# Seven products instead of eight for three more pairs of projection blocks, and z loaded from memory for every second attention head

## The chip, the cores and the metric

The kernel runs on one core of one Trainium2 chip. The metric is the device time of one execution in microseconds (us); the time before is the median of three runs. The core's engines are TensorE (PE in the rows, with its weight loads as PEld), VectorE (DVE), ScalarE (ACT), GpSimd (POOL) and SyncE (SP, which here issues nearly all DMAs). PE adds up its products in PSUM, eight banks of 128 x 512 float32.

## The reference, cut to what matters

```python
h = rmsnorm(x, norm_g)                       # 1024 tokens x 1024
proj = einsum('bsd,de->bse', h, w_in)        # 11280 columns
(a_q, a_k, a_v, a_o, a_z, a_g, b_q, b_k, b_v, b_z, g_a, g_b) = split(proj)
# branch A, mLSTM of 4 heads of width 256
qk = silu(conv5(concat(a_q, a_k)))
y_a = rmsnorm(mlstm_fw(qk, a_v, a_g) + mlstm_bw(qk, a_v, a_g)) * sigmoid(a_o) * silu(a_z)
# branch B, differential attention, 8 heads of width 128 (two score maps of width 64 each)
att = (softmax(q0 @ k0.T * s) - lam * softmax(q1 @ k1.T * s)) @ b_v      # q, k with RoPE
y_b = rmsnorm(att) * (1 - lambda_init) * silu(b_z)
mix = sigmoid(g_a + gb0) * (y_a @ w_branch_a) + sigmoid(g_b + gb1) * (y_b @ w_branch_b)
out = rmsnorm(x + mix @ w_out, final_g)
```

All of it is float32. The kernel reaches that precision with three products for one: each operand is split into a rounded part (names ending in H) and the rest (L), and H·H, H·L and L·H are added.

## The kernel before

**Blocks.** A block is 128 columns of the projection for all 1024 tokens. Done plainly (`proj`, L429) it is two halves of 512 tokens, each 8 contraction blocks x 3 products, so 48 matmuls of 128x512 into the PSUM tiles `pj`, of which there are two.

**Pairs.** Two blocks can be done together as a 2x2 block product with seven products in place of eight (Strassen's scheme in Winograd's form: `pair_units`, L291; the sums of weight blocks come from `load_form`, those of h from the opening, in `TH`/`TL`). A product is 4 contraction blocks x 3 matmuls, so a pair is 84 matmuls of 128x512 where two plain blocks are 96. A sink takes the four quarters of the result (block i, token half j). Sixteen pairs are made this way, all for the mLSTM: q and k (`conv_sink`) and o with z (`oz_sink`). Results leave for DRAM; their working tiles are the six buffers of `big` and six PSUM banks `T`.

**Stages, in order of time.** The opening: normalise, transpose, four gate blocks (branch B's gate, blocks 0 to 3). The sixteen pairs. A prologue of the attention (q, k, z of head 0 and v of heads 0 and 1). The attention's eight heads. Its tail, with gate blocks between. The mLSTM. The rest of the gates, the two branch products, the output.

**A head of the attention** is eight cycles t, one for 128 queries (`da_cycle`). On PE a cycle has S (12 score matmuls, L923, into two double-bank tiles `S` that fill all of S's banks), T (two groups of four transposes of the combined probabilities of the cycle before, L131 `T<-ident,e`), in odd cycles PV (two groups of 12 products, L959), in even ones M (two transposes of the result `att`, for its mean square), and in cycles 4 and 5 G (four transposes each of the row scale of the head before). T, PV, M and G share two PSUM banks, also called `T`. After S, VectorE takes two maxima `nm` (L926), ScalarE two exponentials `e` (L928), VectorE then combines them (L932 to L934). After T, ScalarE makes `pH` (L947) and VectorE `pL` (L948). After M, ScalarE squares (L971). In G the result is multiplied with `zg` = z(1+tanh(z/2)) (L880, L881) and stored to `yb`.

**The fill.** Between these units stand pieces of plain projection: q and k of the next head (`da_proj`; its results go through VectorE, GpSimd `m`, ScalarE `hl` and DMAs into `kst` and `qq`), v of the next two heads (`da_v`), z and gate blocks (`gate_units`). `Weaver.weave` merges the two lists by planned costs and lags; the tuple `FILL` says how many gate blocks a head gets.

**What sets the order.** PE's order is the one that the weaver writes. The other engines and the DMA queues are ordered by the scheduler of the framework, which reckons with costs of its own; each engine then executes strictly in that order.

Of the kernel before, what the change touches and what calls it, by code (L numbers as in the profile page):

```python
# [7 lines left out]
F32 = mybir.dt.float32  # L8
F32R = mybir.dt.float32r
I32 = mybir.dt.int32  # L10
AF = mybir.ActivationFunctionType
ALU = mybir.AluOpType
AX = mybir.AxisListType

S = 1024
# [3 lines left out]
NH_B = 8  # L19
# [15 lines left out]


INF = 1.0e9
FILL = (1, 0, 0, 0, 0, 0, 0, 3)
MM = 0.214
TP = 0.109  # L40

# [68 lines left out]
class Block:  # L110
# [202 lines left out]
    def oz_sink(self, i0):  # L313


        v, a, box = self.v, self.a, {}

        def sink(i, j, ps, rest):
            if "z" not in box:
                box["z"] = self.big("oz")  # L320
            z = box["z"][:, j * 512:(j + 1) * 512]
            first = j not in box
            box[j] = True
            if rest is not None:
                to = self.psA.tile([128, 512], F32, name="pj", tag="pj", bufs=2) if i == j == 1 else ps
                v.tensor_tensor(out=to, in0=ps, in1=rest, op=ALU.add)
                ps = to
            more = lambda out, x, y: v.scalar_tensor_tensor(out=out, in0=x, scalar=1.0, in1=y, op0=ALU.add, op1=ALU.mult)
            if i == 0:
                a.activation(out=z if first else ps, in_=ps, func=AF.Tanh, scale=0.5)  # L330
                if not first:
                    more(z, ps, z)
            else:
                th = self.s0.tile([128, 512], F32, name="tz", tag="tz", bufs=2)
                a.activation(out=th, in_=ps, func=AF.Tanh, scale=0.5)
                more(z if first else ps, th, ps)
                if not first:
                    more(z, z, ps)
            if not first:
                self.q.dma_start(out=self.gd_ml[i0][:, j * 512:(j + 1) * 512], in_=z)  # L340
        return sink

    def conv_sink(self, seg, n):

# [497 lines left out]
    def da_proj(self, h, st):  # L842
        A, v, a, p, q = self.A, self.v, self.a, self.p, self.q
        w1 = self.w1
        fb = lambda x: x.bitcast(F32)
        kA, kB = ("rope", h, 0), ("rope", h, 1)

        def first(half, pa):
            c = slice(half * 512, (half + 1) * 512)
            m = [w1.tile([128, 512], F32, name=f"m{i}", tag=f"m{i}", bufs=1) for i in range(2)]  # L850
            st["m"] = m
            v.tensor_tensor(out=m[0], in0=pa, in1=self.cosT[:, c], op=ALU.mult)
            v.tensor_tensor(out=m[1], in0=pa, in1=self.sinT[:, c], op=ALU.mult)

        def second(half, pb):
            c = slice(half * 512, (half + 1) * 512)
            if half == 0:
                st["k"] = w1.tile([128, 2, S], F32R, name="kst", tag="kst", bufs=2)
            qq = st["q", half] = w1.tile([128, 2, 512], F32R, name="qq", tag="qq", bufs=3)
            m = st["m"]  # L860

            hl = w1.tile([128, 4, 512], F32R, name="hl", tag="hl", bufs=1)
            v.tensor_tensor(out=fb(hl[:, 2]), in0=pb, in1=self.sinT[:, c], op=ALU.mult)
            v.tensor_tensor(out=fb(hl[:, 3]), in0=pb, in1=self.cosT[:, c], op=ALU.mult)
            p.tensor_tensor(out=m[0], in0=m[0], in1=fb(hl[:, 2]), op=ALU.subtract)
            p.tensor_tensor(out=m[1], in0=fb(hl[:, 3]), in1=m[1], op=ALU.add)
            for i in range(2):
                a.copy(hl[:, i, :], m[i])
                p.tensor_tensor(out=hl[:, 2 + i, :], in0=m[i], in1=fb(hl[:, i, :]), op=ALU.subtract)
            for x in range(2):  # L870
                for i, to in enumerate((st["k"][:, :, c], qq)):
                    for j in range(2):
                        r, g = 64 * j + 32 * x, 64 * (1 - i) + 32 * j
                        q.dma_start(out=fb(to[r:r + 32]), in_=fb(hl[g:g + 32, x::2]))

        kz = ("w_in", OFF["bz"] + 128 * h)

        def zz(half, ps):
            st["g", half] = g = w1.tile([128, 512], F32, name="zg", tag="zg", bufs=2)
            a.activation(out=g, in_=ps, func=AF.Tanh, scale=0.5)  # L880
            v.scalar_tensor_tensor(out=g, in0=g, scalar=1.0, in1=ps, op0=ALU.add, op1=ALU.mult)  # L881

        qk = []
        for half in range(2):
            qk += self.proj(kA, half, lambda ps, half=half: first(half, ps))
            qk += self.proj(kB, half, lambda ps, half=half: second(half, ps), name=("qk", h))
        z = self.proj(kz, 0, lambda ps: zz(0, ps)) + self.proj(kz, 1, lambda ps: zz(1, ps), name=("z", h))
        for half in range(2):
            z[(half + 1) * self.PIECES - 1].after = ((("G", h - 1, half), LAG["G"]),)
        return qk, z  # L890
# [538 lines left out]
    def build(self):  # L1429
# [19 lines left out]
        do = lambda f, cost=0.0: Unit(cost, f)  # L1449
        pool = lambda *x, **k: tc.tile_pool(*x, **k)  # L1450
        with pool(name="const", bufs=1) as self.const, \
# [16 lines left out]
            dt = lambda n: [self.dram.tile([128, S], F32, name=f"{n}{i}") for i in range(8)]  # L1468
            self.tg = {"ga": dt("tga"), "gb": dt("tgb")}
            self.ya, self.yb, self.gd_ml = dt("ya"), dt("yb"), dt("gm")  # L1470
            self.cd = {n: dt("c" + n) for n in ("ak", "akH", "akL", "aqH", "aqL")}
            self.pairs, sinks, self.praws, self.f = [], [], {}, {}
            for n in range(NH_A):
                for i, seg in enumerate(("ak", "aq")):
                    self.pairs.append(((seg, 2 * n), (seg, 2 * n + 1)))
                    sinks.append(self.conv_sink(seg, n))
                    self.pairs.append((("ao", 2 * n + i), ("az", 2 * n + i)))
                    sinks.append(self.oz_sink(2 * n + i))
            self.ident = self.const.tile([128, 128], F32, name="ident")
            make_identity(self.nc, self.ident)  # L1480
            self.mhalf = self.const.tile([128, 8], F32, name="mhalf")
            self.v.memset(self.mhalf, -0.5)

            gq = [("gb", i) for i in range(8)] + [("ga", i) for i in range(8)]
            fill = lambda m: sum((self.gate_units(*gq.pop(0)) for _ in range(m)), [])

            def begin():
# [12 lines left out]
            sts = [dict() for _ in range(NH_B)]  # L1500
            stm = [dict() for _ in range(NH_A)]
            st3 = {}
            w = Weaver()
            w.add(enter("h", "hpool"), enter("tab", "tab", side="right"), enter("tf", "tf", side="right"),
                  enter("p0", "p0", side="right"), banks("ps0", T=6), keep(E.PE, E.Activation, E.DVE, E.Pool), do(begin))
            k = self.PIECES
# [37 lines left out]
            w.add(leave("ps0", "s0", "tf"), enter("w1", "w1", side="right"), banks("ps1", S=2, T=2))  # L1544
            w.banks.update(S=1, T=2)
            qk, z = zip(*[self.da_proj(h, sts[h]) for h in range(NH_B)])
            w.add(do(lambda: setattr(self, "ahead", True)), *qk[0], *z[0], *self.da_v(0, sts[0:2]))
            prev = None
            for h in range(NH_B):
                cur = self.da_parts(h, sts[h])  # L1550
                main = sum((self.da_cycle(cur, prev, t) for t in range(8)), [])
                ahead = qk[h + 1] if h + 1 < NH_B else []
                if h + 1 == NH_B:
                    nxt = fill(FILL[h]) + z[h]
                elif h % 2 == 1:
                    nxt = ahead + self.da_v((h + 1) // 2, sts[h + 1:h + 3]) + fill(FILL[h])
                else:
                    nxt = z[h - 1] + ahead + fill(FILL[h]) + z[h] if h else ahead + fill(FILL[0])
                w.weave(main, nxt)
                prev = cur  # L1560
            end = sum((self.da_cycle(None, prev, t) for t in range(6)), [])
# [8 lines left out]
            rest = fill(len(gq))  # L1570
# [17 lines left out]
            k = len(passA) // 2  # L1588
# [52 lines left out]
```

## Time and profile before

| | |
|---|---|
| runs | 1705.68, 1709.62, 1704.77 us; median 1705.68 |
| the profiled execution | 1706.56 us in all, span 1704.7 us from first to last instruction |
| PE, DVE, ACT, POOL busy | 97%, 58%, 46%, 36% of the span |
| matmuls | 9431 |
| mean granted clock of TensorE | 0.994 |
| stages, us from the start | opening to 67; pairs 67 to 398; prologue to 455; heads 0 to 6 455 to 999; head 7 999 to 1067 (its last S); tail to 1124; mLSTM and the rest to 1705 |

The rows give a start and a length in us, the engine, the line of the code, the operation and its operands as out<-in, the shape, a count, and in brackets how long the engine had been idle and what ended that. A matmul's length is longer than its distance to the next one, since they are pipelined; for what one costs the distance counts.

### The profile page before, as it was taken

The numbers are of one execution on the slowest core, as the hardware profiler recorded it, in microseconds if no ns is written. First come the engines' busy times: TensorE is split into PE (matmuls) and PEld (weight loads), VectorE is DVE, ScalarE is ACT, GpSimd is POOL, SyncE is SP. The second block draws the span as 40 slices with busy tenths as digits, with TensorE's granted clock in tenths as the row PEclk, the third lists the DMA queues.
The fourth block names the chain that finished last, engine by engine and source line by source line (L and its number), as shares of the span: only waits on it lengthen the run. The fifth ranks groups of instructions, "written<-read, shape, count | busy, mean of one in ns | idle before, by whom it ended". The sixth has DMA issues, their size and how long they took to land. (4 is left out here: it accounts for less than half of the span.)

```text
span 1704.7 us, 25425 instructions
## 1 busy us (share of the span) xinstructions
PE 1654.3 (97%) x9431; PEld 1389.8 (82%) x9431; DVE 988.3 (58%) x1799; ACT 777.0 (46%) x1554; POOL 606.5 (36%) x680
## 2 busy tenths in 40 slices
PE   7999999999999999999999999999999899999998
PEld 5777887887877987898788878899999777888887
DVE  5778668674377666666666655226666633135533
ACT  7454555553265455454545455325655644022221
POOL 5767676665243134413241331221330312212000
PEclk9999999999999999999999999999999999999999
DMA  5334444334231213221231222175464327344222
GB/s 181 98 121 130 137 123 132 116 124 146 65 81 44 63 38 87 56 69 38 75 81 32 62 62 75 50 208 155 143 170 137 109 89 237 117 147 136 87 91 83
DMA packets 175630, 178.79 MB, mean 105 GB/s; under 512 B 12185, under 2 KB 135410, under 8 KB 175506
## 3 DMA queue, kind: packets, MB, share of 16 engines
q1 hardware_dynamic: 174594, 175.58, 34.5%
q8 instruction: 74, 1.21, 0.3%
q10 hardware_dynamic: 912, 1.59, 0.2%
q14 instruction: 50, 0.41, 0.1%
HBM read 114.11 MB, written 46.24 MB: 94 GB/s over the span
## 5 line engine op out<-in xcount | busy, mean ns | idle before, releaser
L429 PE MATMUL pj<-hH,wH 128*128 128x512 f32 x640 | 266.8, 417 | 3.3 <-ACT f L542 1.5
L429 PE MATMUL pj<-hH,wL 128*128 128x512 f32 x640 | 252.0, 394 | 1.8 <-POOL wL L207 1.8
L429 PE MATMUL pj<-hL,wH 128*128 128x512 f32 x640 | 250.8, 392 | 0.2 <-DVE hL L580 0.2
L209 POOL TENSOR_TENSOR wL<-raw,wH 128x1024 fp32r<-128x1024 f32 x41 | 99.7, 2431 | 291.9 <-ACT wH L204 289.5
L928 ACT ACTIVATE e<-S,nm 128x1024 f32<-128x1024 f32 x128 | 142.5, 1115 | 96.1 <-DVE nm L926 96.0
L926 DVE TENSOR_REDUCE nm<-S 128x1 f32<-128x1024 f32 x128 | 150.5, 1218 | 8.5 <-PE S L923 7.8
L429 PEld LDWEIGHTS pj<-hH,wH 128*128 128x128 f32 x640 | 121.0, 189 | 37.9 <-issue 14.5
L451 PE MATMUL pj<-wH,hH 128*128 128x256 f32 x512 | 149.9, 293 | 0.3
L948 DVE TENSOR_TENSOR pL<-T,pH 128x512 fp32r<-128x512 f32 x128 | 87.9, 689 | 105.8 <-ACT pH L947 104.9
L451 PE MATMUL pj<-wL,hH 128*128 128x256 f32 x512 | 144.8, 283 | 1.4 <-POOL wL L207 1.4
L429 PEld LDWEIGHTS pj<-hH,wL 128*128 128x128 f32 x640 | 120.6, 188 | 30.3 <-POOL wL L207 3.2
L451 PE MATMUL pj<-wH,hL 128*128 128x256 f32 x512 | 144.5, 282 | 0.0
L429 PEld LDWEIGHTS pj<-hL,wH 128*128 128x128 f32 x640 | 121.3, 190 | 18.3 <-DVE hL L580 0.6
L429 PE MATMUL pj<-sl_yb,wH 128*128 128x512 f32 x384 | 121.8, 397 | 4.4 <-ACT sl_yb L1314 2.2
L947 ACT CAST pH<-T 128x512 fp32r<-128x512 f32 x128 | 74.8, 585 | 84.6 <-PE T L131 84.0
L204 ACT CAST wH<-raw 128x1024 fp32r<-128x1024 f32 x56 | 58.9, 1052 | 114.3 <-PE pj L429 88.1
L923 PE MATMUL S<-kst,qq 64*128 64x512 f32 x768 | 106.7, 408 | 0.0
L451 PEld LDWEIGHTS pj<-wH,hH 128*128 128x128 f32 x512 | 97.7, 191 | 5.5 <-issue 2.2
L451 PEld LDWEIGHTS pj<-wL,hH 128*128 128x128 f32 x512 | 97.5, 190 | 2.3 <-POOL wL L207 2.3
L451 PEld LDWEIGHTS pj<-wH,hL 128*128 128x128 f32 x512 | 97.7, 191 | 0.1
L429 PEld LDWEIGHTS pj<-sl_yb,wH 128*128 128x128 f32 x384 | 73.3, 191 | 22.5 <-DVE sl_yb L1315 3.3
L923 PEld LDWEIGHTS S<-kst,qq 64*128 64x128 f32 x768 | 67.8, 184 | 26.3 <-issue 10.5
(358 smaller groups left out, 4112.2 us busy)
## 6 DMA issues: line engine op xcount, KB each, us to landing
raw<-in_w_in_dram SPq DMA_DIRECT2D x88, 512.0 KB, 3.9
kst<-hl SPq DMA_DIRECT2D x64, 128.0 KB, 2.4
qq<-hl SPq DMA_DIRECT2D x64, 128.0 KB, 2.4
x<-in_x_dram SPq DMA_DIRECT2D x8, 512.0 KB, 6.1
cak<-y SPq DMA_DIRECT2D x16, 256.0 KB, 2.3
cakH<-cin SPq DMA_DIRECT2D x16, 256.0 KB, 4.4
cakL<-tz SPq DMA_DIRECT2D x16, 256.0 KB, 4.1
gm<-oz SPq DMA_DIRECT2D x16, 256.0 KB, 2.7
```

The lines of the kernel that those rows point to most:

```text
L204: self.a.copy(wH, raw)
L209: self.p.tensor_tensor(out=wL, in0=raw, in1=wHf, op=ALU.subtract)
L429: self.t.matmul(ps, lhsT=l[:, k, :], rhs=r, start=(n == 0), stop=(n == 23))
L451: self.t.matmul(ps[:, i, :], lhsT=l, rhs=r[:, k, :], start=(kh == 0 and k == 0 and m == 0), stop=(kh == 1 and k == 3 and m == 2))
L923: self.t.matmul(ps[:, o], lhsT=qq[r, x, c], rhs=k[r, y, o], start=(m == 0), stop=(m == 2))
L926: v.tensor_reduce(out=nm, in_=ps, axis=AX.X, op=ALU.max, negate=True)
L928: a.activation(out=e, in_=ps, func=AF.Exp, bias=nm[:, 0:1], accum_out=Z[:, j, t:t + 1])
L947: a.copy(pH[:, :, s], ps)
L948: v.tensor_tensor(out=pL[:, :, s], in0=ps, in1=pH[:, :, s].bitcast(F32), op=ALU.subtract)
```

## The change

Six blocks leave the attention and become three pairs between the mLSTM's: (gate B 4, gate B 5) after the first four pairs, (z of head 1, z of head 3) after eight pairs, (z of head 5, z of head 7) after twelve. Two sinks are new. `gate_sink` does the tanh and stores the gate where `gate_units` stored it. `z_sink` does tanh, then (1+tanh)·z, and stores to new DRAM tiles `gz`. In odd heads `da_proj` returns, in place of 16 pieces of product, two units that load z (`zg<-gz`); they stand behind the last G of the head before, since `zg` has two buffers. z of head 0 moves from the prologue into head 0, where the gate block 4 was. `FILL` for head 7 becomes 2.

So the fill of a head, in blocks of 48 matmuls (q and k count as 2, v of two heads as 2), is: head 0 q,k + z0 (3, as before); odd heads to 5 q,k + v (4, as before); heads 2, 4, 6 q,k + z (3, before 4); head 7 two gate blocks (2, before 4).

```diff
-FILL = (1, 0, 0, 0, 0, 0, 0, 3)
+FILL = (0, 0, 0, 0, 0, 0, 0, 2)
...
+    def stored_sink(self, to, finish):
+        box = {}
+        def sink(i, j, ps, rest):
+            if i not in box:
+                box[i] = self.big("out")
+            out = box[i][:, j * 512:(j + 1) * 512]
+            if rest is not None:
+                sums = self.psA.tile([128, 512], F32, name="pj", tag="pj", bufs=2) if i == j == 1 else ps
+                self.v.tensor_tensor(out=sums, in0=ps, in1=rest, op=ALU.add)
+                ps = sums
+            finish(out, ps, i)
+            self.q.dma_start(out=to[i][:, j * 512:(j + 1) * 512], in_=out)
+        return sink
...
+    def z_sink(self, heads):
+        def finish(out, ps, i):
+            self.a.activation(out=out, in_=ps, func=AF.Tanh, scale=0.5)
+            self.v.scalar_tensor_tensor(out=out, in0=out, scalar=1.0, in1=ps, op0=ALU.add, op1=ALU.mult)
+        return self.stored_sink([self.gz[h] for h in heads], finish)
...
+        def load_z(half):
+            st["g", half] = g = w1.tile([128, 512], F32, name="zg", tag="zg", bufs=2)
+            q.dma_start(out=g, in_=self.gz[h][:, half * 512:(half + 1) * 512])
+        if h % 2 == 1:
+            return qk, [Unit(0.0, lambda half=half: load_z(half)) for half in range(2)]
...
+                if n < 3:
+                    blocks = (("gb", 4), ("gb", 5)) if n == 0 else (("bz", 4 * n - 3), ("bz", 4 * n - 1))
+                    self.pairs.append(blocks)
+                    sinks.append(self.gate_sink(blocks) if n == 0 else self.z_sink([h for _, h in blocks]))
...
-            w.add(do(lambda: setattr(self, "ahead", True)), *qk[0], *z[0], *self.da_v(0, sts[0:2]))
+            w.add(do(lambda: setattr(self, "ahead", True)), *qk[0], *self.da_v(0, sts[0:2]))
...
                 if h + 1 == NH_B:
-                    nxt = fill(FILL[h]) + z[h]
+                    nxt = fill(FILL[h])
                 elif h % 2 == 1:
-                    nxt = ahead + self.da_v((h + 1) // 2, sts[h + 1:h + 3]) + fill(FILL[h])
+                    nxt = ahead + self.da_v((h + 1) // 2, sts[h + 1:h + 3])
                 else:
-                    nxt = z[h - 1] + ahead + fill(FILL[h]) + z[h] if h else ahead + fill(FILL[0])
+                    nxt = ahead + z[h]
+                if h % 2 == 1:
+                    k = [i for i, u in enumerate(main) if u.name and u.name[0] == "G"][-1] + 1
+                    main[k:k] = z[h]
                 w.weave(main, nxt)
```

Two places show how the order moves. The first is PE in head 7 from cycle 6 to the S of cycle 7. Before, between S of cycle 6 and S of cycle 7 (`pj` is fill, `att` is M, `e` with its number is T):

```order
L923 MATMUL S<-kst,qq 128x512 x12
L429 MATMUL pj<-hH_170,wH 128x512
L429 MATMUL pj<-hL_172,wH 128x512
L429 MATMUL pj<-hH_170,wL 128x512
...
L131 MATMUL T<-ident,att 128x128 x2
L131 MATMUL T<-ident,e_10211 128x128 x4
...
L131 MATMUL T<-ident,e_10211 128x128 x4
L923 MATMUL S<-kst,qq 128x512 x12
```

The left-out rows are fill too: nine matmuls ahead of M in all, and twelve between the two groups of T. The same place now, from the transposes that end cycle 5:

```order
L131 MATMUL T<-ident,e_10280 128x128 x8
L960 MATMUL S<-kst,qq 128x512 x12
L131 MATMUL T<-ident,att 128x128 x2
L131 MATMUL T<-ident,e_10360 128x128 x8
L960 MATMUL S<-kst,qq 128x512 x12
```

No fill is left between the two S, and in the cycles 5 and 7 on either side there is none either (the fill of head 7 ends in cycle 4). ScalarE's order at this place is now two `e` of cycle 5, `att`, two `pH`, two squares, one `pH`, two `e` of cycle 6, one `pH`, two `e` of cycle 7, `att`, two `pH`.

The second place is ScalarE in head 2, where the second half of the next head's q and k passes through it (`hl`), and `wH` are weights being split. Before, at cycle 6:

```order
L961 COPY att<-T 128x256
L947 CAST pH<-T 128x4x128
L193 CAST wH<-raw 128x8x64 x2
L947 CAST pH<-T 128x4x128
L868 CAST hl<-m_6092 128x512
L868 CAST hl<-m_6093 128x512
L928 ACTIVATE e_6259,Z<-S,nm 128x1024
```

Now, at cycle 5:

```order
L984 CAST pH<-T 128x4x128
L193 CAST wH<-raw 128x8x64 x2
L899 CAST hl<-m_6347 128x512
L984 CAST pH<-T 128x4x128
L899 CAST hl<-m_6348 128x512
L965 ACTIVATE e_6497,Z<-S,nm 128x1024
```

The step moved one cycle earlier, and the second `pH` of the cycle before, which stood ahead of both `hl`, now stands between them. GpSimd does two `wL` there ahead of the two `m` from which `hl` is copied; in head 6 one of these is a whole block (128x1024). Behind the attention's tail all five orders are as before, row for row.

More of the change, by code (lines that the diff above doesn't have):

```diff
@@ L341, in oz_sink, with gate_sink, finish @@
         return sink
+    def stored_sink(self, to, finish):
[11 more added lines that the diff above has]
+        return sink
+    def gate_sink(self, blocks):
+        idx = [(0 if seg == "ga" else 8) + i for seg, i in blocks]
+        def finish(out, ps, i):
+            self.a.activation(out=out, in_=ps, func=AF.Tanh, scale=0.5, bias=self.gbh[:, idx[i]:idx[i] + 1])
+        return self.stored_sink([self.tg[seg][i] for seg, i in blocks], finish)
+    def z_sink(self, heads):
+        def finish(out, ps, i):
+            self.a.activation(out=out, in_=ps, func=AF.Tanh, scale=0.5)
+            self.v.scalar_tensor_tensor(out=out, in0=out, scalar=1.0, in1=ps, op0=ALU.add, op1=ALU.mult)
+        return self.stored_sink([self.gz[h] for h in heads], finish)
     def conv_sink(self, seg, n):
@@ L1470, in build @@
             self.ya, self.yb, self.gd_ml = dt("ya"), dt("yb"), dt("gm")
+            self.gz = {h: self.dram.tile([128, S], F32, name=f"gz{h}") for h in range(1, NH_B, 2)}
             self.cd = {n: dt("c" + n) for n in ("ak", "akH", "akL", "aqH", "aqL")}
@@ L1482, in build @@
             self.v.memset(self.mhalf, -0.5)
-            gq = [("gb", i) for i in range(8)] + [("ga", i) for i in range(8)]
+            gq = [("gb", i) for i in (0, 1, 2, 3, 6, 7)] + [("ga", i) for i in range(8)]
             fill = lambda m: sum((self.gate_units(*gq.pop(0)) for _ in range(m)), [])
```

## The prediction

> **What bounds the kernel now.** I read the stages first, as a table of busy time by stretch (start:end, length, then busy us of PE, PEld, DVE, ACT, POOL, the granted clock, the DMA share, GB/s), then PE's waits in the attention.
>
> ```profile
> 67.00:398.00 331.00, 326.19 (x1410) 257.91 (x1409) 242.42 (x368) 174.85 (x315) 221.91 (x197) 1.00 0.41 126
> 398.00:455.00 57.00, 55.59 (x334) 49.54 (x333) 12.27 (x21) 11.14 (x21) 19.91 (x14) 1.00 0.34 93
> 455.00:999.00 544.00, 538.08 (x3447) 447.35 (x3446) 356.60 (x493) 274.43 (x572) 182.20 (x172) 1.00 0.24 63
> 999.00:1067.00 68.00, 68.00 (x403) 54.65 (x401) 40.55 (x53) 35.87 (x74) 14.59 (x13) 1.00 0.20 63
> ...
> PE T L131 <- ACT T L971: 5.6, 6, 1.4
> ```
>
> PE is never idle in head 7 (68.00 of 68.00) and idle 5.9 us in 544 in the heads before; 5.6 of that is one wait, transposes T held up by ScalarE's squares, which occupy one of the two banks. No other engine is over 73% in any of these stages. So PE sets the time in every stage that the change touches: matmuls saved are time saved, until the fill is too thin for the chains that it covers.
>
> **Fewer matmuls.** What a matmul of fill costs, by the distance of starts: 36 in a row in the opening; a short run of six in the attention up to the PV behind it; and the 84 of one pair (two rows, a pair apart).
>
> ```profile
> 47.42 0.39 PE L429 MATMUL pj<-hH,wH 128*128 128x512 f32 x1
> ...
> 55.59 0.24 PE L131 MATMUL T<-ident,rows 89*128 89x89 f32 x1
> ...
> 1068.53 0.50 PE L429 MATMUL pj<-hH,wH 128*128 128x512 f32 x1
> ...
> 1070.02 0.28 PE L959 MATMUL T<-pH,vH 128*128 128x256 f32 x1
> ...
> 316.79 0.40 PE L291 MATMUL T<-TH,wH 128*128 128x512 f32 x1
> ...
> 336.23 0.40 PE L291 MATMUL T<-TH,wL 128*128 128x512 f32 x1
> ```
>
> That is 8.17/36 = 0.227 us in a long run, 1.49/6 = 0.248 in a short one (its first matmul follows another kind), and 19.44 for a pair. Removed are 6 blocks of 48. The prologue loses one, in long runs: 48 x 0.227 = 10.9. Heads 2, 4, 6 lose one each and head 7 with its tail two: 240 matmuls at 0.227 to 0.248, 54.5 to 59.5; runs of three to twelve are usual there, so the middle, 57.0. Added are three pairs, 58.3. Sum: 58.3 - 67.9 = **-9.6** (bounds -7.1 and -12.1).
>
> **What the pairs need beside PE.** By the stage's row DVE is busy 242 us in 331, POOL 222. A new pair has no convolution: four tanh, four (1+tanh)z, three additions, and seven forms of weights. The average pair, with half a convolution, needs 242/17 = 14 us of DVE and 13 of POOL per 19.4, so the new ones fit. Their stores are 256 KB each, as the sinks of o and z have; the six `big` tiles are shared with two more results a pair, and the convolution before has a whole pair (o, z) to let go of its own. PE idled 331.00 - 326.19 = 4.8 in the 16 pairs, 0.3 each: **+0.9** for three more (bounds 0 and 2). Two late waits may go:
>
> ```profile
> 391.57 0.50 PE L291 MATMUL T<-TH,wH 128*128 128x512 f32 x1 [0.68 <-ACT u L298]
> 395.26 0.50 PE L291 MATMUL T<-hH,wL 128*128 128x512 f32 x1 [0.63 <-DVE pj L326]
> ...
> 426.89 0.50 PE L429 MATMUL pj<-hH,wH 128*128 128x512 f32 x1 [1.41 <-DVE zg L881]
> ```
>
> The first two lie beside the last pieces of the sine table on ScalarE and VectorE; those now run three pairs before the end, where they can meet other work: **-0.5** (0 to -1.3). The third is the prologue's: VectorE took the z of head 0 ahead of the rope products whose bank PE waited for. That z leaves the prologue, and what follows there is v, over 20 us of PE: **-0.9** (0 to -1.4).
>
> **The new loads.** Eight loads of 256 KB wait on SP for the `yb` store that frees `zg`, and what is queued behind, the next raw weights, waits with them.
>
> ```profile
> yb<-zg SPq DMA_DIRECT2D x16, 256.0 KB, 2.5
> ```
>
> Two such stores hold SP some 5 us per odd head. The raw weights behind are fetched at least a block of fill (11 us) ahead, and z is used a head's fill later, so I take 0; the cover would be gone if a G came late enough to push the load behind the next qq. GpSimd's product with `zg` stands ahead of weight splits and would then hold those.
>
> **Head 7: the fill ends.** What a cycle needs without fill, from the last S before, which has little beside it:
>
> ```profile
> 1066.42 0.60 PE L131 MATMUL T<-ident,e 128*128 128x128 f32 x4
> 1066.94 1.66 PE L923 MATMUL S<-kst,qq 64*128 64x512 f32 x12
> ...
> 1067.11 0.58 ACT L947 CAST pH<-T 128x512 fp32r<-128x512 f32 x1
> 1067.85 0.68 DVE L948 TENSOR_TENSOR pL<-T,pH 128x512 fp32r<-128x512 f32 x1
> 1068.63 2.36 DVE L926 TENSOR_REDUCE nm<-S 128x1 f32<-128x1024 f32 x2
> 1069.89 1.12 ACT L928 ACTIVATE e<-S,nm 128x1024 f32<-128x1024 f32 x1 [2.20 <-DVE nm L926]
> ...
> 1072.04 0.19 ACT L928 ACTIVATION_READ_ACCUMULATOR e<-S,nm 128x1 f32 x1
> 1072.77 1.28 DVE L934 SCALAR_TENSOR_TENSOR e<-e,r,e 128x1024 f32<-128x1024 f32 x1
> 1074.42 0.37 ACT L961 COPY att<-T 128x256 f32<-128x256 f32 x1 [2.20 <-PE T L959]
> ```
>
> From the start of S its banks are free after 1072.23 - 1066.94 = 5.3 us and the probabilities ready after 7.1. On PE, S takes 1.6, four transposes 0.5, M 0.25, PV 2.8 (24 at 0.118). Cycles 0 to 4 keep 7.4 us and more of PE work; cycles 5, 6, 7 have 5.9, 2.9 and 5.4. Walking the new order with these durations, from S of cycle 5 at 0: G, PV, first T at 4.9; the second T waits for PV's bank, which ScalarE empties behind its exponentials (5.65, wait 0.25). S of cycle 6 at 6.15 to 7.75. The two `pL` of that T end at 7.8 and 8.5, behind the combination at 7.1; so M waits 0.1 and the next T 0.45, until 9.55. The maxima of S 6 start at 8.5, its exponentials end at 12.2, and S of cycle 7 waits until then: 2.65. PV follows; the last T waits again for PV's bank, which is copied behind the exponentials of S 7 (18.9), 1.75. Together **+5.2**. Bounds: 2.65, if the bank waits vanish; and three full chains of 7.1 less the PE work of 14.2, 7.1.
>
> **Even heads: one wait for another.**
>
> ```profile
> 667.38 0.66 PE L131 MATMUL T<-ident,e 128*128 128x128 f32 x4 [1.13 <-ACT T L971]
> 827.45 0.66 PE L131 MATMUL T<-ident,e 128*128 128x128 f32 x4 [1.12 <-ACT T L971]
> 987.81 0.66 PE L131 MATMUL T<-ident,e 128*128 128x128 f32 x4 [1.42 <-ACT T L971]
> ...
> 493.71 2.81 POOL L194 TENSOR_TENSOR wL<-raw,wH 128x512 fp32r<-128x512 f32 x2 [5.79 <-PE T L131]
> 496.48 1.28 POOL L865 TENSOR_TENSOR m<-m,hl 128x512 f32<-128x512 f32 x1
> ...
> L209 POOL TENSOR_TENSOR wL<-raw,wH 128x1024 fp32r<-128x1024 f32 x41 | 99.7, 2431 | 291.9 <-ACT wH L204 289.5 <-PE T L291 2.4
> ```
>
> In heads 2, 4, 6 the squares came late in cycle 6, since `hl` held ScalarE. These waits, 3.7 in all, go: the step is now in cycle 5. But there the second `pH` stands behind one `hl` (behind both in head 6). From the end of the second rope product: weight copies 0.7, two `wL` 2.8, `m` 1.3, `hl` 0.6, `pH` 0.6, `pL` 0.7, so the bank is free at about 6.5. PE reaches PV, which needs it, after nine matmuls, T, S, G and three more, 5.4: 1.1 of wait, twice. In head 6 the split is 2.4 with a 1.05 copy before it, and both `hl` come first, 8.2: 2.8. Net 5.0 - 3.7 = **+1.3** (bounds -3.7 and +5.0).
>
> **Sum.** -9.6 + 0.9 - 0.5 - 0.9 + 0 + 5.2 + 1.3 = -3.6. The profiled execution, 1706.56, becomes 1703.0. It was 0.9 above the median, so 1702.1 in runs like those shown, -0.2%. A change of 0.3% (5.1 us) is about what a measurement of this kernel can tell from none, so the bounds are 1700.6 and 1710.8.
>
> **Rivals.** *The saving arrives whole (B).* If the scheduler's order on ScalarE bites less than walked, only the S wait of 2.65 stays and the old waits go: -9.6 + 2.65 - 1.4 - 0.5 + 0.9 = -8, 1697.7. For it: head 0, with the fill that even heads get now, took 518.92 - 455.61 = 63.3 us, 7.9 a cycle, without a wait of over 0.4. Against: the two bank waits follow from orders that are fixed.
>
> ```profile
> 455.61 1.66 PE L923 MATMUL S<-kst,qq 64*128 64x512 f32 x12
> 518.92 1.66 PE L923 MATMUL S<-kst,qq 64*128 64x512 f32 x12
> ...
> 658.91 1.66 PE L923 MATMUL S<-kst,qq 64*128 64x512 f32 x12
> 667.96 0.50 PE L923 MATMUL S<-kst,qq 64*128 64x512 f32 x2
> ...
> 1361.89 0.48 PE L131 MATMUL T<-ident,W 128*128 128x128 f32 x1 [2.72 <-DVE W L1185]
> 1360.00:1367.00 7.00, 5.11 (x18) 4.53 (x19) 1.83 (x4) 1.17 (x3) 0.69 (x2) 0.55 0.46 145
> ```
>
> *The clock falls in head 7 (C).* In the mLSTM a wait of 2.72 stands in a stretch of 7 us whose granted clock was 0.55. Head 7 gets a wait of 2.65 with little around it. The same loss, 7 x 0.45 = 3.2, gives 1705.3. [...]
>
> *Slower (D): even heads become bound by the chain.* Cycle 6 of head 2, where `hl` held ScalarE, took 667.96 - 658.91 = 9.05. If all 24 cycles of heads 2, 4, 6 took that in place of 8.5 (80 less 11.4 by eight), 24 x 0.55 = 13 is added: 1715. It decides from 8.9 a cycle on. Against it: head 0's 7.9.
>
> *Nothing saved.* The new order has 9395 matmuls against 9431, 36 fewer, so the products do go.
>
> **Chances.** A, as summed, 0.50 (1698.5 to 1706); B 0.29; C 0.13; D 0.08. Of A about a seventh lies below 1700.6. Faster by over 0.3%: 0.29 + 0.07 = 0.36; within: 0.43 + 0.12 = 0.55; slower: 0.09. The range leaves out D and the lower part of B: 1695.5 to 1707.5.
>
> **What would show it.** Each S of head 7 about 6 us apart in cycles 5 and 6, with a wait of 2 to 3 us ahead of the last; even heads 68 to 70 us, with the wait at PV in cycle 5; 19.4 us per new pair; no wait of `pj` in the prologue. It is wrong if the pairs lose more than 1 us each, or if PE waits at rope products or `zg`.

## Result and the profile after

The changed kernel takes 1715.74 us (median of 6 runs, 1714.09 to 1717.45) where before takes 1705.73 (6 runs): a ratio of 1.0053 (95% interval 1.004 to 1.0066). By the ratio it is 9 us slower, between the medians 10. I had forecast 1702.1, most likely no difference that can be told, and a range of 1695.5 to 1707.5. The profiled execution took 1714.09 us with a span of 1712.3, the one of before 1706.56 with 1704.7; the sums between before and after below are made between these two spans.

First the same table by stretch as in the prediction, of the kernel after: the pairs, the prologue, heads 0 to 6, head 7 up to its last S (start:end, length, busy us of PE, PEld, DVE, ACT, POOL, granted clock, DMA share, GB/s). Below it are PE's waits in heads 0 to 6 (waited for, us in total, times, longest).

```profile
67.00:455.00 388.00, 384.74 (x1663) 305.30 (x1662) 265.27 (x398) 199.50 (x358) 253.70 (x221) 1.00 0.39 123
455.00:499.00 44.00, 44.00 (x285) 40.34 (x284) 8.99 (x16) 9.05 (x17) 17.80 (x13) 1.00 0.42 116
499.00:1024.70 525.70, 510.92 (x3304) 423.51 (x3303) 351.66 (x489) 269.04 (x564) 182.07 (x170) 0.99 0.25 64
1024.70:1079.10 54.40, 52.19 (x327) 41.17 (x325) 39.93 (x51) 30.81 (x66) 12.19 (x13) 1.00 0.21 69
```

```profile
PE T L996 <- DVE pL L985: 5.0, 6, 2.4
PE T L131 <- ACT T L1008: 4.1, 6, 1.4
PE T L996 <- ACT pH L984: 3.8, 3, 1.3
PE T L131 <- ACT att L998: 1.8, 3, 0.6
```

In heads 0 to 6 PE was idle 5.9 us before; now it is idle 525.70 - 510.92 = 14.8. Most of the new waiting is PV (L996) held up by `pH` or `pL`. By stages, cut at the start of the first product of a pair, at the first S of each head and at the first transposes of the mLSTM (`T<-ident,akf`) in the two traces:

| stage | before | after | difference | forecast |
|---|---|---|---|---|
| opening | 67.8 | 67.4 | -0.4 | 0 |
| pairs and prologue | 387.8 | 432.0 | +44.2 | +46.9 |
| head 0 | 63.3 | 62.7 | -0.6 | 0 |
| heads 1, 3, 5 | 240.6 | 240.5 | -0.1 | 0 |
| heads 2, 4, 6 | 240.0 | 222.3 | -17.7 | -32.9 |
| head 7 and the tail | 125.1 | 109.2 | -15.9 | -17.6 |
| mLSTM and the rest | 580.2 | 578.1 | -2.0 | 0 |

(Of the forecast's 57.0 for five blocks, 34.2 belong to heads 2, 4, 6 and 22.8 to head 7 and the tail.) One row carries the miss: 15 us that were to come from heads 2, 4 and 6 did not.

What happens there is the same three times. The timeline of head 2, cycle 3, in the kernel after (start, length, engine, line, operation):

```profile
666.46 1.68 POOL L147 TENSOR_TENSOR rb_y<-rb_v,mhalf 128x8 f32<-128x8 f32 x1
...
667.74 0.60 PE L131 MATMUL T<-ident,e 128*128 128x128 f32 x4
...
668.50 1.14 POOL L149 TENSOR_TENSOR rb_w<-rb_w,rb_v 128x8 f32<-128x8 f32 x1
...
670.50 1.28 POOL L896 TENSOR_TENSOR m<-m,hl 128x512 f32<-128x512 f32 x1
671.74 1.29 POOL L897 TENSOR_TENSOR m<-hl,m 128x512 f32<-128x512 f32 x1
...
671.81 0.62 ACT L899 CAST hl<-m 128x512 fp32r<-128x512 f32 x1 [4.46 <-POOL m L896]
673.06 0.62 ACT L899 CAST hl<-m 128x512 fp32r<-128x512 f32 x1 [0.62 <-POOL m L897]
673.58 0.58 ACT L984 CAST pH<-T 128x512 fp32r<-128x512 f32 x1
...
674.19 0.69 DVE L985 TENSOR_TENSOR pL<-T,pH 128x512 fp32r<-128x512 f32 x1 [4.62 <-ACT pH L984]
...
674.21 0.39 PE L996 MATMUL T<-pH,vH 128*128 128x256 f32 x1 [1.28 <-ACT pH L984]
674.94 0.39 PE L996 MATMUL T<-pL,vH 128*128 128x256 f32 x1 [0.34 <-DVE pL L985]
```

The transposes T from which the second `pH` is made end at 668.3. ScalarE is idle from 667.4 to 671.8, and yet that `pH` starts at 673.58. It stands behind the two `hl` in ScalarE's order, these wait for GpSimd's `m`, and `m` starts only when the row scale `rb` of the head before is done. PE reaches the second half of PV and waits 1.28 + 0.34. In the kernel before, z of the odd head stood ahead of q and k in the fill of an even head (`z[h - 1] + ahead` in the diff). This half of q and k passed one cycle later, in cycle 4, about 10 us after the last `rb` operation (30.4 us from the start of head 2):

```profile
699.91 1.28 POOL L865 TENSOR_TENSOR m<-m,hl 128x512 f32<-128x512 f32 x1 [3.94 <-DVE hl L863]
```

That is 40.3 us after the head's start; in the changed kernel it is 28.2, right behind the row scale. So taking that z out moved the step into the cycle of the row scale. In cycle 5 the second half of q and k comes by and costs 0.84, 0.83 and 2.35 in the three heads.

Behind such waits the granted clock fell. The following rows cut the trace at about the edges of that stretch in head 4:

```profile
824.04:827.45 3.41, 1.79 (x13) 1.39 (x12) 0.89 (x2) 1.72 (x3) 3.41 (x4) 1.00 0.00 0
827.45:830.86 3.41, 3.41 (x15) 3.01 (x16) 2.08 (x3) 2.44 (x5) 0.40 (x1) 0.54 0.77 175
```

After 3.41 us in which PE was idle for 1.62 came 3.41 us with the clock at half (the second row starts 0.3 us ahead of the recorded edge, so 0.54). The fill's matmuls start 0.43 us apart in it (829.46, 829.89, 830.31) and 0.23 behind it (831.62, 831.85, 832.08). So about half of 3.41 is lost, 1.7 us, an estimate from that clock and the stretch's length. The records of the kernel after hold three such stretches in the attention and its end, from 827.8, 1001.8 and 1080.3; those of before hold none ahead of 1360.

### The profile page after: what moved, and what is told of

Same layout as the page of the kernel before. It is cut to its first block, busy times and chain, and to the rows that moved or that the text cites. A ratio compares the mean times of both kernels' runs of the same rounds, so it can differ in the third digit from the quotient of the medians.

```text
span 1712.3 us, 25475 instructions
## 1 busy us (share of the span) xinstructions
PE 1651.9 (96%) x9395; PEld 1384.6 (81%) x9395; DVE 1003.2 (59%) x1817; ACT 789.2 (46%) x1578; POOL 630.7 (37%) x698
## 5 line engine op out<-in xcount | busy, mean ns | idle before, releaser
L460 PE MATMUL pj<-hH,wH 128*128 128x512 f32 x544 | 227.7, 419 | 1.9 <-ACT f L573 1.5
L460 PE MATMUL pj<-hH,wL 128*128 128x512 f32 x544 | 214.3, 394 | 1.8 <-POOL wL L207 1.8
L460 PE MATMUL pj<-hL,wH 128*128 128x512 f32 x544 | 213.4, 392 | 0.2 <-DVE hL L611 0.2
L965 ACT ACTIVATE e<-S,nm 128x1024 f32<-128x1024 f32 x128 | 142.4, 1114 | 75.2 <-DVE nm L963 74.5
L209 POOL TENSOR_TENSOR wL<-raw,wH 128x1024 fp32r<-128x1024 f32 x35 | 85.2, 2434 | 235.8 <-ACT wH L204 231.1
L460 PEld LDWEIGHTS pj<-hH,wH 128*128 128x128 f32 x544 | 102.8, 189 | 32.2 <-issue 13.8
L460 PEld LDWEIGHTS pj<-hH,wL 128*128 128x128 f32 x544 | 102.4, 188 | 26.3 <-POOL wL L207 3.4
L460 PEld LDWEIGHTS pj<-hL,wH 128*128 128x128 f32 x544 | 103.1, 189 | 15.8 <-DVE hL L611 0.6
L204 ACT CAST wH<-raw 128x1024 fp32r<-128x1024 f32 x50 | 52.5, 1050 | 123.4 <-PE pj L460 103.6
L291 PE MATMUL T<-TH,wL 128*128 128x512 f32 x304 | 102.5, 398 | 2.9 <-ACT u L298 2.2
L291 PE MATMUL T<-TH,wH 128*128 128x512 f32 x304 | 102.8, 398 | 0.0
```

The lines of the kernel that those rows point to most:

```text
L204: self.a.copy(wH, raw)
L209: self.p.tensor_tensor(out=wL, in0=raw, in1=wHf, op=ALU.subtract)
L291: self.t.matmul(ps, lhsT=l[:, k, :], rhs=r[:, k, :], start=(first and k == 0 and m == 0), stop=(k == 3 and m == 2), skip_group_check=not f ...
L460: self.t.matmul(ps, lhsT=l[:, k, :], rhs=r, start=(n == 0), stop=(n == 23))
L965: a.activation(out=e, in_=ps, func=AF.Exp, bias=nm[:, 0:1], accum_out=Z[:, j, t:t + 1])
```

## Experiments

Ten kernels ran, in three groups (e, f and g). Each group had its own runs of before (medians 1705.55, 1708.07 and 1707.19), so ratios to those are compared and not raw times.

**e1: `hl` by GpSimd.** The changed kernel with

```diff
-                a.copy(hl[:, i, :], m[i])
+                p.tensor_copy(out=hl[:, i, :], in_=m[i])
```

> The changed kernel with one line edited: in da_proj the copy m -> hl is done by GpSimd, not by ScalarE, in all heads. TensorE's, VectorE's issue orders stay. Theory 1 (order on ScalarE: in heads 2, 4, 6 the second pH of a step stands behind the hl copies, which wait for GpSimd's m): the waits at PV in cycles 3 and 5 of these heads, 1.62 three times and 0.84, 0.83, 2.35, together 8.9 us, go, and with them the stretches of half clock at 828 and 1002 (1.7 us each): 1714 less 12, so 1702, at most 1704 if the clock falls elsewhere. Theory 2 (with three blocks of fill the chain of a cycle, S to pH, bounds these heads whatever ScalarE's order): the waits come back at S, T or PV, less than 3 us are gained, 1711 or more. GpSimd's copy takes about 1.3 us where ScalarE's took 0.62, hidden in both theories.

Measured: 1704.72 us, ratio 0.999 (0.9981 to 0.9999). With one copy moved (in all heads) the 9 us are gone. PE's waits from the end of the prologue to the end of head 6:

```profile
PE T L131 <- ACT T L1008: 2.3, 3, 1.4
PE pj L482 <- DVE hl L895: 2.2, 1, 2.2
PE T L131 <- ACT att L998: 1.8, 3, 0.6
```

The waits at PV are gone, 8.9 us, and so are both stretches of half clock in heads 4 and 6. Heads 2, 4, 6 take 70.0, 69.1, 69.0 (73.2, 73.8, 75.2). GpSimd's row scale is where it was, and `m` and `hl` are as late as ever, but the second `pH` no longer stands behind them (head 2, cycle 3):

```profile
671.75 0.59 ACT L984 CAST pH<-T 128x512 fp32r<-128x512 f32 x1 [1.02 <-PE T L131]
...
673.88 1.28 POOL L896 TENSOR_TENSOR m<-m,hl 128x512 f32<-128x512 f32 x1
675.23 0.61 POOL L899 CAST hl<-m 128x512 fp32r<-128x512 f32 x1
```

TensorE's order was the same row for row. So the heads with three blocks of fill are not bound by the chain of a cycle: theory 2 (and rival D of the prediction) falls. The total missed the 1702 mainly because head 0's step in the prologue now made v wait 2.16 us (second row above), with a stretch of half clock behind it, at 486.1; f2 below leaves head 0 out.

**e2: the row scale by VectorE.**

```diff
-                rs = self.rsqrt(w1, st["ms"], 1.0 / 128.0, zz, "rb", eng=p)
-                p.tensor_scalar(out=rs, ...)
+                rs = self.rsqrt(w1, st["ms"], 1.0 / 128.0, zz, "rb")
+                v.tensor_scalar(out=rs, ...)
```

> The changed kernel with the row scale of a head (the six small operations rb, all but the power) done by VectorE, not by GpSimd. Theory 1 as above, with GpSimd's row scale as the reason that the first step of q and k is late in cycle 3 (m waits 1.6 us behind it): the waits of 1.62 at PV in cycle 3 of heads 2, 4, 6 shrink to under 0.3 each and the half clock at 828 goes, those of cycle 5 (0.84, 0.83, 2.35) stay: 1714 less 4 to 6.5, so 1707.5 to 1710. If the row scale is not the reason, cycle 3 waits as before: 1713 to 1716.

Measured: 1717.21 us, ratio 1.0064 (1.0052 to 1.0077): no gain, and above both forecasts. The row scale was a reason for the late `pH`, but moving it made something else late. Head 2, cycle 3:

```profile
667.32 1.24 DVE L148 TENSOR_TENSOR rb_w<-rb_y 128x8 f32<-128x8 f32 x1 [0.84 <-POOL rb_y L147]
...
670.47 2.39 DVE L971 SCALAR_TENSOR_TENSOR e<-e,r,e 128x1024 f32<-128x1024 f32 x1
672.79 1.22 DVE L151 TENSOR_TENSOR rb_y<-rb_y,rb_w 128x8 f32<-128x8 f32 x1
673.93 0.68 DVE L985 TENSOR_TENSOR pL<-T,pH 128x512 fp32r<-128x512 f32 x1
...
670.49 3.50 POOL L900 TENSOR_TENSOR hl<-m,hl 128x512 fp32r<-128x512 f32 x2
...
671.09 0.58 ACT L984 CAST pH<-T 128x512 fp32r<-128x512 f32 x1
...
674.66 0.38 PE L996 MATMUL T<-pL,vH 128*128 128x256 f32 x1 [2.14 <-DVE pL L985]
```

`pH` came 2.5 us earlier, as theory 1 has it, and PE's wait for it went. But `pL` is now behind products of VectorE that lie beside GpSimd's, and these were slow: the combination of the probabilities took 2.39 us (1.28 in the prediction's row), a product of eight columns 1.24. PE waited 2.14 for `pL` in place of 1.62. So this run shows that the row scale made `pH` late, but not what the kernel would gain without it.

**e3: the pairs of z alone, heads 2, 4, 6 full.**

```diff
-FILL = (0, 0, 0, 0, 0, 0, 0, 2)
+FILL = (0, 0, 1, 0, 1, 0, 1, 2)
-                if n < 3:
+                if n in (1, 2):
-            gq = [("gb", i) for i in (0, 1, 2, 3, 6, 7)] + ...
+            gq = [("gb", i) for i in range(8)] + ...
-                    nxt = ahead + z[h]
+                    nxt = fill(FILL[h]) + ahead + z[h]
```

> Only the two pairs of z, as in the change; the gate blocks 4 and 5 stay plain products and, with one gate block from behind the mLSTM, give heads 2, 4, 6 one block each ahead of q and k, so that these have four blocks again. Head 7 keeps two. Against the changed kernel: one pair less (-19.4), two blocks more (+22 to 23). If the loss lies in heads 2, 4, 6 alone (theories 1 and 2), their waits fall from 12.9 to about the 3.7 of before and the two stretches of half clock there go (3.4): 1714 + 3 - 9.2 - 3.4 = 1704.5 (1702 to 1707). If it lies in the pairs or in the loads of z, 1715 or more.

Measured: 1719.2 us, ratio 1.0081 (1.0068 to 1.0094). The part on the heads held: 2, 4, 6 took 79.9, 79.9, 80.2 and PE waited there as before the change (1.12, 1.12, 1.41). The total did not: pairs and prologue took 419.4 us, 12.6 less than in the changed kernel where a whole pair of 19.4 was left out, and the mLSTM and the rest, without one gate block (11 us), were shorter by 2.0 only. Where the 6.8 went in the pairs, the next run shows. In the rest, PE was idle for 24.9 us where it was for 19.7 in the changed kernel, and the clock was at half for 17.07 us in a row from 1436.5, where the changed kernel has 3.41. PE's waits in e3 from 1400 to 1460 are mostly for `sl_yb`, an operand of the branch products (2.1 and 1.5 in the changed kernel for these two rows):

```profile
PE pj L460 <- ACT sl_yb L1351: 6.6, 4, 4.1
PE pj L460 <- DVE sl_yb L1352: 3.7, 5, 2.1
```

So the gate block was probably cover there too (no run tests it), and the total of e3 does not tell what the two pairs of z are worth.

**e4: the pair of gate blocks alone** (z of all heads in the attention as before, z of head 0 in head 0).

```diff
-                if n < 3:
+                if n == 0:
-        if h % 2 == 1:
+        if False:
             return qk, [Unit(0.0, lambda half=half: load_z(half)) for half in range(2)]
...
-                    nxt = fill(FILL[h])
+                    nxt = fill(FILL[h]) + z[h]
...
-                    nxt = ahead + z[h]
-                if h % 2 == 1:
+                    nxt = z[h - 1] + ahead + z[h] if h else ahead + z[h]
+                if False:
```

> Only the pair of gate blocks; z of every head is computed in the attention as before, z of head 0 in head 0 where the gate block 4 was, head 7 has three blocks (before four, changed kernel two). Theory 1 and 2 (the loss lies in heads 2, 4, 6): these heads are as before, so against before 19.4 is added, the prologue gives 10.9 + 1.4, head 7 gives 11.4, the pairs' waits change by 0 to -1.5: -4.3 to -6, so 1700.5 to 1702.5 where before is 1706.5. If a pair without convolution or the thinner head 7 costs more than counted, 1705 or more.

Measured: 1708.97 us, ratio 1.0023 (1.0013 to 1.0034), slower than before. Heads 1 to 6 are those of before to 0.1 us; against the forecast of 1700.5 to 1702.5 the loss is in the pairs. PE's waits in that stage, which read the same in e3, and VectorE at the longest of them:

```profile
PE T L291 <- DVE gc_emt L846: 3.4, 1, 3.4
...
PE T L131 <- DVE gc_sint L846: 1.7, 1, 1.7
```

```profile
293.32 1.15 DVE L663 TENSOR_SCALAR wk<-wk 128x256 f32<-128x256 f32 x1
295.49 0.69 DVE L407 SCALAR_TENSOR_TENSOR y<-tz,pj 128x512 f32<-128x512 f32 x1 [1.02 <-ACT tz L405]
296.09 0.75 DVE L404 SCALAR_TENSOR_TENSOR pj<-cin,cols,pj 128x512 f32<-128x512 f32 x1
296.75 0.30 DVE L846 COPY gc_emt<-T 128x32 f32<-128x32 f32 x2
```

The copies out of the banks of small transposes (the mLSTM's gates, "columns") stand behind the convolution, with operations on `wk`, for the sine table, between. These pieces are set among the products of the pair with index 10. With one more pair ahead (e4), or with the first added pair after eight (e3), index 10 is a pair of o with z and the convolution of the pair before runs beside it; before the change, and with the pairs as the change puts them, index 10 is a pair of q or k.

**f3: the same with these pieces at index 11.**

```diff
-((10, 5), 2, columns)
+((11, 5), 2, columns)
```

> The gate pair alone as in its first run, with one number changed: the pieces of the mLSTM's gates called columns stand among the products of the twelfth pair (index 11) and not the eleventh. With the added pair the eleventh is one of o with z, while VectorE still does the convolution of the one before; the copies that empty the bank of these transposes stood behind that convolution, and PE waited 1.74 and 3.38 us with a stretch of half clock behind each. At index 11 they stand beside a pair of q or k again, as before the change. Theory 3 (position of these pieces): the two waits and both stretches go, 6 to 7 us: 1708.97 - 6.5 = 1702.5 (1701 to 1704). If a pair without convolution is itself the cause, 1707 or more.

Measured: 1703.64 us, ratio 0.9977 (0.9967 to 0.9988). Both waits and both stretches of half clock are gone; pairs and prologue take 395.9 us, not 401.8, with one new wait of 1.85, for an addition that stands behind operations on `wk` on VectorE. So the gate pair costs about what it should once that meeting is avoided, and 0.2% remains as a gain.

**f1 and f2: the edit of e1 on both kernels**, for heads 1 to 7, head 0 left to ScalarE.

```diff
-                a.copy(hl[:, i, :], m[i])
+                (a.copy if h == 0 else p.tensor_copy)(hl[:, i, :], m[i])
```

> The kernel before with the copy m -> hl done by GpSimd for heads 1 to 7 (head 0, in the prologue, stays with ScalarE). It shows what of the 11 us that this edit took off the changed kernel belongs to the change. Theory 1 (hl on ScalarE holds what stands behind it): before loses only its own waits, 1.13, 1.12, 1.42 in heads 2, 4, 6 and 0.64 each in 1, 3, 5: 5.6 us, so 1700 (1699 to 1701.5). If the squares of before were late for another reason, 1703.5 or more. If the edit helps any kernel by 10 us, whatever the waits, 1696 or less.

> The changed kernel with the same edit for heads 1 to 7. The first run of this edit, for all heads, got a new wait of 2.16 at v in the prologue and a stretch of half clock behind it, 4.1 in that stage; with head 0 left to ScalarE this goes: 1704.7 - 4.1 = 1700.6 (1699 to 1703). Against the kernel before with this edit it says what the change is worth once ScalarE holds nothing: by my sum of dense work -9.6, less the waits that head 7, the tail and the last cycles of the even heads showed (about 3 + 4 + 3): between -4 and +1. If it is worth the -9.6, theory 1 explains the whole miss.

Measured: f1 1700.18 us, ratio 0.9953 (0.9936 to 0.997); f2 1701.18 us, ratio 0.9957 (0.9941 to 0.9974). The two rows are heads 0 to 6 of f1 and then of f2:

```profile
455.50:998.00 542.50, 542.50 (x3481) 452.19 (x3481) 366.93 (x498) 264.36 (x549) 210.97 (x201) 1.00 0.25 63
```

```profile
499.50:1007.60 508.10, 504.79 (x3303) 420.72 (x3302) 360.58 (x489) 255.15 (x536) 205.78 (x198) 1.00 0.26 66
```

In f1 PE never waits. On equal terms the change is worth nothing: the spans are 1698.7 and 1699.4. By stages f2 less f1 is +44.6 for pairs and prologue (+47.4 in products), -28.2 for heads 2, 4, 6 (34.2 of products left out, as forecast), -15.1 for head 7 and tail (22.8 left out), -0.7 elsewhere. So theory 1 explains the 9 us against before, but not the whole distance to my dense sum of -9.6: 6.0 stay in the even heads and 7.7 at the end of the attention.

The two traces divide the 6.0. In the even heads f2's PE is idle for 3.3 us, f1's never. The 144 matmuls of fill that are gone take 32.9 us off the distances between starts, 0.229 each, not 34.2. And the transposes T of the probabilities start 1.6 us farther apart in all.

**g1 and g2: what the end of the attention loses.** Both are f2 with one further edit. g1 weaves head 7 in two halves, one block of fill in each; g2 takes a gate block from the tail into head 7.

```diff
+                if h + 1 == NH_B:
+                    c = [i for i, u in enumerate(main) if u.name and u.name[0] == "S"][4]
+                    w.weave(main[:c], nxt[:len(nxt) // 2])
+                    w.weave(main[c:], nxt[len(nxt) // 2:])
+                else:
+                    w.weave(main, nxt)
```

```diff
-FILL = (0, 0, 0, 0, 0, 0, 0, 2)
+FILL = (0, 0, 0, 0, 0, 0, 0, 3)
-            w.weave(end[:-2], fill(2))
+            w.weave(end[:-2], fill(1))
```

> The changed kernel with hl by GpSimd in heads 1 to 7 (1701.2 in its run), and in head 7 the two blocks of fill shared out: one woven into cycles 0 to 3, one into cycles 4 to 7, so that cycles 3, 6 and 7 have little or none, not 5, 6 and 7 in a row. Theory 4 (it is the row of bare cycles: 0.80, 1.08 and 0.30 of wait within 4 us, and 6.8 us of half clock behind them, 3.4): waits of two cycles do not fall into one stretch of 3.4 us, the half clock goes, and 0 to 1 us of waits: 1697 (1696 to 1699). If the chain of each thin cycle costs its wait wherever it stands, the waits come at cycle 3 too and nothing is gained: 1700.5 or more.

> The same base (1701.2), with one gate block moved from the tail into head 7 (three blocks there, one less behind the last S); the matmuls of the whole stay the same. With three blocks head 7 showed no wait (61.4 us in the run of the gate pair). If the tail's chains are covered by what is left, head 7 and tail take 61.4 + 53.6 - 10.9 = 104 in place of 110.0: 1695.3; with up to 4 us of new waits in the thinner tail, 1695 to 1699.5. If the tail needs that block as much as head 7, 1700.5 or more: then this block of fill cannot be saved at all and its 11 us were never there to gain.

Measured: g1 1702.52 us, ratio 0.9971 (0.9959 to 0.9982); g2 1699.37 us, ratio 0.9954 (0.9941 to 0.9966). Spreading did not help: theory 4 falls. PE's waits in head 7 and tail are, first in f2, then in g1's head 7 and in g2 (its first row lies behind the tail, in the mLSTM):

```profile
PE S L960 <- ACT e L965: 1.4, 2, 1.1
PE T L131 <- DVE pL L985: 1.0, 2, 0.8
PE T L131 <- ACT att L998: 0.8, 2, 0.6
```

```profile
PE T L131 <- ACT T L1008: 4.1, 1, 4.1
PE T L131 <- ACT att L998: 1.7, 2, 1.1
```

```profile
PE T L127 <- ACT kwH L1118: 1.7, 1, 1.7
PE T L131 <- POOL vL L1096: 1.4, 1, 1.4
PE T L131 <- ACT att L998: 0.7, 1, 0.7
```

In g1 the squares that free the bank for T stand behind two exponentials and a gate's tanh on ScalarE (M ends at 1059.8):

```profile
1060.33 1.11 ACT L965 ACTIVATE e<-S,nm 128x1024 f32<-128x1024 f32 x1
...
1062.52 0.68 ACT L868 ACTIVATE gt<-pj,gbh 128x512 f32<-128x512 f32 x1
1063.09 0.28 ACT L1008 ACTIVATE T<-T 128x128 f32<-128x128 f32 x1
...
1063.84 0.29 ACT L1008 ACTIVATE T<-T 128x128 f32<-128x128 f32 x1
```

That is the old trouble in a new place: with thin fill it is again ScalarE's order that PE meets. g2 gets the waits out of head 7: head 7 and tail take 61.4 + 44.3 = 105.7 us in its profile where f2 took 110.0. Two waits stay in its thinner tail, the 1.4 and the 0.7. In the runs its ratio cannot be told from f2's.

**f4: the gate pair with the pieces at index 11 and `hl` by GpSimd in heads 1 to 7.**

> The third kernel of this call with the edit of the first one (hl by GpSimd in heads 1 to 7). Its heads 1 to 6 are those of before, so theory 1 takes off the same 5.6: 1702.5 - 5.6 = 1697 (1695 to 1699.5), faster than both kernels. If the two edits meet somewhere, 1700 or more.

Measured: 1698.63 us, ratio 0.9945 (0.9928 to 0.9961); faster than before and the changed kernel, as are f1, f2, f3, g1 and g2. Against f3 the edit took off 5.0 of the 5.6 expected.

## Why the prediction was wrong, step by step

- **Matmuls saved: right.** The pairs cost 58.4 us (252 products, from the starts in the trace, without waits) where 58.3 was counted, and the prologue lost 11.2, without its wait, where I had 10.9.
- **Pairs' waits: one sign wrong, small.** Forecast +0.9 - 0.5 in the pairs and -0.9 in the prologue. Waits fell from 4.8 to 3.2 in the pairs, so the +0.9 had the wrong sign, and from 1.4 to 0 in the prologue. That the three pairs went in so smoothly was also a matter of position: e3 and e4 put one pair fewer ahead of the gate pieces and lost 6 to 7 us there. I had not looked at that.
- **Loads of z: right at 0.** The odd heads, which load it, took 240.5 us where they took 240.6.
- **Even heads, +1.3: the step that failed.** I walked one half of q and k, in cycle 5, and there got 1.1, 1.1, 2.8 where 0.84, 0.83, 2.35 came. The first half, in cycle 3, I did not walk, and so put its wait at nothing. There GpSimd has the row scale ahead of `m`, and the wait was 1.62 in each head, 4.9 in all. Nor did the old waits for the squares go as I said: 1.39, 0.40, 0.43 stayed, at another cycle, and 0.59 each came at the last T. Together 12.9 us of waits less 3.7 before: +9.2. With the two stretches of half clock (3.4) that is +12.6 in place of +1.3. The clock's share shows in the heads themselves: less its waits, head 2, without half clock, took 68.7 us, heads 4 and 6, with one stretch each, 70.4 and 70.3. Of the 15.2 that were missing, 3.9 remain. By f2 against f1 above, 1.3 of these are fill that was cheaper than my 0.2375 a matmul and 1.6 are transposes that start farther apart; the last us I cannot divide.
- **Head 7, +5.2: right in size, its parts not.** Head 7 and tail lost 7.0 of the 22.8. Waits were 2.9 (0.78 and 0.16 at M and T, 1.08 and 0.60 at S, the rest small), not 5.2: the wait of 2.65 at the last S came as 1.08 + 0.60, and PV's bank cost 0.25 where I had 0.25 and 1.75. The clock added 1.7. The other 2.3 are no waits: mostly transposes and PV products that start farther apart, while the fill was worth 23.0 as against 22.8 forecast. The rows of the last S:

```profile
1079.29 0.50 PE L960 MATMUL S<-kst,qq 64*128 64x512 f32 x1 [1.08 <-ACT e L965]
1080.38 2.92 PE L960 MATMUL S<-kst,qq 64*128 64x512 f32 x11 [0.60 <-ACT e L965]
```

- **Rival C: right mechanism, one of three places.** I gave the half clock to head 7 alone, at 3.2. It came three times, 5.1 us in all, twice in the even heads. The row of the prediction, with its wait of 2.72, was the right guide: waits that add up to 1.62, 2.09 and 1.69 us within one interval of 3.41 were followed by half clock. The chance of 0.13 that I gave it was my estimate alone.
- **Rival D: right number (1715), wrong mechanism.** It had all 24 cycles of the even heads bound by the chain at 9 us each. (Its price was also a little high: 80 less 11.4 by eight is 8.6 and not 8.5, so 11 and not 13, which gives 1713.5.) e1 excludes it: the same order of TensorE ran these heads in 69 to 70 us. The loss sat in two or three cycles per head, behind one instruction in one queue.

What stays open: why the transposes start farther apart where fill is thin, and the last us in the even heads.

## What to carry to other kernels

When fill is taken from a stage, walk every step that shares an in-order engine with the critical copies, in all its places, and ask what stands *behind* the one that waits for a third engine; here a 0.6 us copy that waited for GpSimd held the `pH` of the softmax. Taking cover away exposes such orders. Mending the order (here by giving the copy to the engine that it waits for) made the kernel before 0.47% faster (f1), and the products saved added nothing to that (f2, 0.43%). So try the same mending on the kernel before: only that told what the change itself was worth.

## What the hardware showed beyond that

**Half clock came in stretches of 3.41 us, behind idle time of TensorE.** In all twelve traces the stretches of half clock last 3.41 us or a multiple of it (the last one is cut by the end of the trace), and within one execution they start on one grid: in the kernel after 51, 74, 160, 181 and 258 times 3.413 us behind the first, in before 10, 22 and 100 times. I divided each trace from the pairs on by that grid and added up PE's idle time per interval at full clock. Of the 48 intervals with 1.0 to 1.45 us of idle time, 2 were followed by half clock; of the 24 with 1.45 to 1.84, 12; of the 28 with more, all. In the traces of before and after alone it was 1 of 12, 2 of 4 and 7 of 7. Under 2 us of idle time were enough: 1.62 and 1.69 in the kernel after. The same wait was followed by half clock or not: that of 1.28 + 0.34 was in head 4, with 1.62 in one interval, and was not in heads 2 and 6, where an interval's edge left 1.22 of it in one and where it came to 1.57. The spread of the changed kernel's runs goes with the clock too: three at 1714.1 to 1714.8 have a mean clock of 0.994 and three at 1716.7 to 1717.5 one of 0.992: 0.002 x 1712 = 3.4 us, where the means of the two lie 2.7 us apart and the clock is given to 0.001. What decides between 1.45 and 1.84 us is not known.

**Some products of VectorE and GpSimd that lay side by side took longer.** Beside GpSimd's products of two operands, VectorE's combination took 2.39 us in place of 1.28 (e2), and a product of eight columns 1.24, where the next one, at 669.16, took 0.14 (GpSimd was idle from 668.55 to 669.25). The other way, GpSimd's product of eight columns took 1.14 us in the row of 668.50, of which 1.07 lay beside VectorE's combination, and 0.20 at 668.22, 669.72 and 670.00; that combination took 1.29. Over the twelve traces, the 501 combinations that met no work of GpSimd took 1.28 to 1.29 us each; of the 267 that met some, 116 took over 1.4. In the traces of before and after alone it was 96 of 1.28 to 1.29, and 6 of 32 over 1.4.

**A copy on GpSimd is cheap.** I had put 1.3 us for it, like its products; the cast of 128x512 took 0.61 us in the median of the 32 in e1 (at most 1.61), as long as ScalarE's 0.62.
